# Attention weights from differences of the scan's neighbouring columns, and a new deal of the last block's side work

## The chip, the cores and the metric

The kernel runs on one core of one Trainium2 chip. The metric is the device time of one execution in microseconds (us); times are the median of several executions. TensorE (PE in the profile, PEld for its weight loads) does the matrix products, VectorE (DVE), ScalarE (ACT) and GpSimd (POOL) the elementwise work, and SyncE (SP) issues the DMA transfers.

## The reference

One layer of a hybrid decoder on x of 2048 positions by 1024 channels, in float32. x is normalised and modulated, and one input projection gives the columns of three token mixers. Their gated outputs are put side by side, go through one output projection and are added to x.

```python
proj = h @ w_in                      # columns au av az | bq bk bv bo bz bi bf | cq ck cv cz
y_a = spatial_gating_branch(ga_u, ga_v, ...) * silu(ga_z)        # branch A: 4 groups x 64
q_b, k_b = split(silu(causal_conv(concat(mb_q, mb_k))))          # branch B: mLSTM, 4 heads x 96
h_b = rms_norm(mlstm_branch(q_b, k_b, mb_v, mb_i, mb_f), ...)
y_b = sigmoid(mb_o) * h_b * silu(mb_z)
# branch C: stick-breaking attention, 6 heads x 64, for each block of 128 queries
z = einsum('bthd,bshd->bhts', qb, kb) * scale
log_not = where(strict, log_sigmoid(-z), 0.0)
suffix = cumsum(log_not, axis=3, reverse=True) - log_not
a = where(strict, exp(log_sigmoid(z) + suffix), 0.0)
outs.append(einsum('bhts,bshd->bthd', a, vb))
y_c = h_c * silu(sc_z)
x = x + gate * (concat([y_a, y_b, y_c]) @ w_out)
```

With b = sigmoid(-z) (1 where masked) and R(s) the product of b over all columns from s on, the weight of column s is sigmoid(z) times R(s+1). Since sigmoid(z) = 1 - b, that is R(s+1) - R(s).

## The kernel before

The 2048 positions are 16 tiles of 128. They are worked through in three blocks of 5, 5 and 6 tiles (`BLOCKS`). In each block the six attention heads come in three pairs (`p` = 0, 1, 2). For each pair, `c_proj` projects the pair's q, k and v for the block's tiles (a lead of some tiles first, four in the last block; the rest later), `c_evac` norms and stores them in `Kst`, `Vst` and `Qst`, and `stick` does the attention. Products are done in a split form: every operand is a rounded part and a remainder, so that one projection step of 384 columns is three matmuls (L297 to L299), eight steps to a tile.

`stick` cuts each tile's keys into units of up to four blocks of 128; a pair of the last block has 44 units. A unit goes through four steps, each one unit behind the step before it in the list. `front`: two matmuls write z into PSUM (L401, L402; two buffers), ScalarE writes bb = sigmoid(-z) (L406) and be = sigmoid(z) (L407), GpSimd sets the masked corner of the diagonal unit in bb to 1 (L409) and in be to 0 (L411), VectorE turns bb into its running product from the right (L414, a scan that carries on from the unit before), and be becomes be times bb shifted by one column (L418, in turn on VectorE and on GpSimd). `middle`: TensorE transposes be (L429) into a PSUM tile "at" (two buffers, taken in program order), ScalarE rounds it into aT (L431), VectorE writes the remainder (L432). `back`: TensorE multiplies with Vst (L444). `fin` folds the pair's two heads and sends them out.

The projections of the other branches are the side work. Each is a generator that yields after each projection step; the last block has eight such chunks of 48 steps: `bqk_proj` halves 0 and 1, `bg_proj` halves 0 and 1, `cz_proj`, `a_proj` halves 0 and 1, and `bv_proj`. `interleave` writes out the program: after each step of a pair's attention it lets the side work advance in proportion to the costs given. A scheduler that simulates the engines then sets the order on each engine, by priority among what is ready; attention has a small priority over the rest. So side work that was written late can run early, where TensorE has nothing else.

Before, the last block's chunks were dealt 3, 3 and 1 to the pairs, and `bv_proj` followed behind the last pair (`tail`). `mix` threads small work into a chunk: `gating` (branch B's gate terms for all tiles) into the first pair's side work and `first_chunk` (the first mLSTM tile) into the second's. `a_proj` keeps its gated values in two tiles with one buffer each, `va` and `gu`, which are used again by the next half, after its spatial products (L580, which take an "at" tile) and its DMA to y_d (L586).

After the last block all pools are closed, and the final part lays its tiles over their memory: the output weights are loaded into `wst` (L1026, over the projection weights `wr` and the activations `hT`) and split into `wo` (L901, L902), while mLSTM tiles and the output projection `out_proj` (L995 to L997) run.

Of the kernel before, what the change touches and what calls it, by code (L numbers as in the profile page):

```python
# [12 lines left out]
AF = mybir.ActivationFunctionType  # L13
ALU = mybir.AluOpType
# [19 lines left out]
def hybrid_block_kernel(ctx: ExitStack, tc: tile.TileContext, x, c, norm_g, w_ada, b_ada, w_in,  # L34
# [344 lines left out]
    def stick(p, t0, nb):  # L379
        units = []  # L380
        for j in range(nb):
            for h in range(2):
                s1 = t0 + j + 1
                while s1 > 0:
                    s0 = (s1 - 1) // 4 * 4
                    units.append((t0 + j, j, h, s0, s1))
                    s1 = s0
        carry = {}
        acc = {}
        outs = {}  # L390
        st = {}
        st_count = []

        def front(u):
            i, j, h, s0, s1 = u
            need[0](j)
            w = (s1 - s0) * P
            nm = f"{p}_{i}_{h}_{s0}"
            z = pz.tile([P, 512], F32, tag="z", name=f"z{nm}")
            kk = Kst[:, h, s0 * P:s1 * P]  # L400
            nc.tensor.matmul(z[:, :w], lhsT=Qst[:, j, 0, h, :], rhs=kk, start=True, stop=False)  # L401
            nc.tensor.matmul(z[:, :w], lhsT=Qst[:, j, 1, h, :], rhs=kk, start=False, stop=True)  # L402
            bb = stk.tile([P, 513], F32, tag="bb", bufs=4, name=f"bb{nm}")
            be = stk.tile([P, 512], F32, tag="be", bufs=4, name=f"be{nm}")
            nc.gpsimd.memset(bb[:, w:w + 1], 1.0)  # L405
            nc.scalar.activation(bb[:, :w], z[:, :w], AF.Sigmoid, scale=-1.0)  # L406
            nc.scalar.activation(be[:, :w], z[:, :w], AF.Sigmoid)  # L407
            if s1 == i + 1:
                nc.gpsimd.affine_select(out=bb[:, w - P:w], in_=bb[:, w - P:w], pattern=[[-1, P]],  # L409
                                        compare_op=ALU.is_gt, fill=1.0, base=0, channel_multiplier=1)  # L410
                nc.gpsimd.affine_select(out=be[:, w - P:w], in_=be[:, w - P:w], pattern=[[-1, P]],  # L411
                                        compare_op=ALU.is_gt, fill=0.0, base=0, channel_multiplier=1)
            rev = bb[:, 0:w + 1][:, ::-1]
            nc.vector.tensor_tensor_scan(rev, rev, rev, carry.get((i, h), 1.0), ALU.mult, ALU.bypass)  # L414
            carry[i, h] = bb[:, 0:1]
            eng = nc.gpsimd if len(st_count) % 2 else nc.vector
            st_count.append(0)
            eng.tensor_tensor(be[:, :w], be[:, :w], bb[:, 1:w + 1], ALU.mult)  # L418
            st[u] = [be, None]
            return 2 * w / 2.4  # L420

        def middle(u):
            i, j, h, s0, s1 = u
            nm = f"{p}_{i}_{h}_{s0}"
            be = st[u][0]
            nb_ = s1 - s0
            at = pat.tile([P, 4, P], F32, tag="at", name=f"at{nm}")
            for s in range(nb_):
                nc.tensor.transpose(at[:, s, :], be[:, s * P:(s + 1) * P], ident)  # L429
            aT = stk.tile([P, 4, 2, P], F32R, tag="aT", bufs=4, name=f"aT{nm}")  # L430
            nc.scalar.copy(aT[:, :nb_, 0, :], at[:, :nb_, :])  # L431
            nc.vector.tensor_tensor(aT[:, :nb_, 1, :], at[:, :nb_, :], aT[:, :nb_, 0, :].bitcast(F32), ALU.subtract)  # L432
            st[u][1] = aT
            return nb_ * 109

        def back(u):
            i, j, h, s0, s1 = u
            aT = st.pop(u)[1]
            if s1 == i + 1:
                acc[i, h] = pav.tile([P, 4, P], F32, tag="av", name=f"av{p}_{i}_{h}")[:, 0:2, :]  # L440
            av = acc[i, h]
            nb_ = s1 - s0
            for s in range(nb_ - 1, -1, -1):
                nc.tensor.matmul(flat(av), lhsT=Vst[:, s0 + s, h, :], rhs=flat(aT[:, s]),  # L444
                                 start=(s0 + s == i), stop=(s0 + s == 0))
            if s0 == 0:
                t1 = stk.tile([P, P], F32, tag="avs", name=f"avs{p}_{i}_{h}")
                nc.scalar.copy(t1, av[:, 1, :])
                t2 = stk.tile([P, P], F32, tag="avt", name=f"avt{p}_{i}_{h}")
                nc.vector.tensor_tensor(t2, av[:, 0, :], t1, ALU.add)  # L450
                outs[i, h] = t2
            return nb_ * 109

        def fin(u):
            i, j, h, s0, s1 = u
            if s0 != 0 or h != 1:
                return 0
            py = flat(pat.tile([P, 4, P], F32, tag="at", name=f"py{p}_{i}"))
            for hh in range(2):
                nc.tensor.matmul(py[:, hh * 64:(hh + 1) * 64], lhsT=outs.pop((i, hh)), rhs=fold, start=True, stop=True)  # L460
            yc = stk.tile([P, P], F32, tag="yc", bufs=1, name=f"yc{p}_{i}")
            nc.scalar.copy(yc, py[:, 0:P])
            nc.sync.dma_start(y_d[i * P:(i + 1) * P, 256 + p * P:256 + (p + 1) * P], yc)
            return 430

        N = len(units)
        for n in range(N + 4):
            for lag, fn in ((0, front), (2, middle), (3, back), (4, fin)):
                if 0 <= n - lag < N:
                    yield fn(units[n - lag])  # L470
# [37 lines left out]
    def bv_proj(t0, nb):  # L508
        with prio(HIGH[0]):
            wt = weights(w_in[0], [(OFF["bv"], 384)])  # L510
        for j in range(nb):
            i = t0 + j
            ps = pproj.tile([P, 512], F32, tag="proj", name=f"pv{i}")
            yield from proj_tc(ps[:, :384], wt, j, 384)
            vb = t512(f"vb{i}")
            vv = vb[:, 0:388].rearrange("p (h e) -> p h e", h=4)
            nc.gpsimd.memset(vv[:, :, 96:97], 1.0)
            nc.scalar.copy(vv[:, :, 0:96], ps[:, :384].rearrange("p (h e) -> p h e", h=4))
            nc.sync.dma_start(vb_d[i * P:(i + 1) * P, :], vb[:, 0:388])
# [230 lines left out]
    def run(g):  # L750
        for _ in g:
            pass

    def chain(*gens):
        for g in gens:
            yield from g

    def mix(a, n, g):
        for m, c in enumerate(a):
            yield c  # L760
            if m % n == n - 1:
                yield next(g, 0)
        yield from g
# [75 lines left out]
    for b, nb in enumerate(BLOCKS):  # L839
        last = b == len(BLOCKS) - 1  # L840
        chunk = nb * KT * 3 * 384 / 2.4
        HIGH[0] = 0 if b == 0 else -4000
        fillers = [
            (chain(bqk_proj(t0, nb, 0), bqk_proj(t0, nb, 1), bg_proj(t0, nb, 0)), 3),
            (chain(bg_proj(t0, nb, 1), cz_proj(t0, nb), a_proj(t0, nb, 0)), 3),
            (a_proj(t0, nb, 1), 1),
        ]
        if b == 1:
            fillers[0] = (mix(fillers[0][0], 8, gate_gemv()), 3)
        if last:  # L850
            fillers[0] = (mix(fillers[0][0], 36, gating()), 3)
            fillers[1] = (mix(fillers[1][0], 14, first_chunk()), 3)
        for p in range(3):
            lead = min(nb, 2 + b)
            if p > 0:
                ready[0] = -1
                cp = c_proj(b, t0, nb, p)
                for _ in range(lead * KT + 1):
                    next(cp)
            cp_cost = 0 if b == 0 and p == 0 else (nb - lead) * KT * 3 * 384 / 2.4  # L860
            if b == 0 and p == 0:
                HIGH[0] = -400
            if p == 2 and not last:
                get_x(t0 + nb, 0)
                get_x(t0 + nb + 1, 1)
            interleave(stick(p, t0, nb), stick_cost(t0, nb), behind(cp, fillers[p][0]), cp_cost + fillers[p][1] * chunk)
        tail = bv_proj(t0, nb)
        if last:
            run(tail)
        else:  # L870
            t1, n1 = t0 + nb, BLOCKS[b + 1]
            ready[0] = -1
            cp = c_proj(b + 1, t1, n1, 0)
            lead = min(n1, 3 + b)
            for m, _ in enumerate(chain(tail, islice(cp, lead * KT + 1))):
                j = m // KT - 1
                if 0 <= j < n1 and m % KT in (1, 5):
                    if m % KT == 1 and j + 2 < n1:
                        get_x(t1 + j + 2, j + 2)
                    hT_half(t1 + j, j, m % KT // 4)  # L880
        t0 += nb
# [200 lines left out]
```

## Time and profile before

| | |
|---|---|
| median of 3 runs | 1473.57 us (1471.72 to 1475.42) |
| the profiled execution: its own time | 1471.23 us |
| its span, first to last instruction | 1469.2 us |
| mean granted TensorE clock | 0.988 |
| busy in the span: TensorE, VectorE, ScalarE, GpSimd | 95%, 69%, 46%, 44% |

The profile is one execution. Busy time is that of an engine's instructions; matmuls overlap and their ends are modelled, so a fully busy TensorE can still have room. Idle time is put down to what released the engine. The stretches named below are in microseconds from the span's start. The last block's attention lies at 727.8 to 893.1 (pair 0), 903.4 to 1062.2 (pair 1) and 1076.3 to 1209.4 (pair 2).

### The profile page before, as it was taken

Reading aid. Unit: us, or ns where it says so; the run is one execution under the profiler, and the core shown is the slowest. Engines: PE = TensorE matmul, PEld = TensorE weight load, DVE = VectorE, ACT = ScalarE, POOL = GpSimd, SP = SyncE. Lnnn points to the kernel's source line nnn. Section 1 sums busy time; section 2 is a strip of 40 time slices with the busy share of each in tenths; the row PEclk is TensorE's granted clock in tenths of the full one; section 3 lists DMA queues with packets and bytes.
Section 4 is the critical chain, followed back from the end, with each engine's and each line's share of the span. In section 5 each row is a group of like instructions: output and inputs, shape, how many; then the busy total and the mean of one; then the engine's idle time right before and its main releaser. Section 6 shows DMA issues by size and latency. Waiting matters only on the chain.

```text
span 1469.2 us, 24957 instructions
## 1 busy us (share of the span) xinstructions
PE 1393.4 (95%) x8468; PEld 1298.2 (88%) x8468; DVE 1018.8 (69%) x1778; ACT 676.5 (46%) x1656; POOL 647.6 (44%) x1140
## 2 busy tenths in 40 slices
PE   5999999898999999999999999999999978999998
PEld 3789999798999999988999899989999867888887
DVE  6797554676995666588799976778778788444543
ACT  3364454453554444346467655556455655111110
POOL 4473553743433432554343343434445337435442
PEclk8999999999999999999999999999999999999999
DMA  9866776666535533633433344303432435555541
GB/s 324 293 204 206 237 228 197 208 202 236 191 128 176 198 116 124 222 100 127 148 105 126 104 146 137 102 15 120 157 102 69 156 113 153 178 160 154 175 154 58
DMA packets 187103, 233.19 MB, mean 159 GB/s; under 512 B 22714, under 2 KB 160344, under 8 KB 186976
## 3 DMA queue, kind: packets, MB, share of 16 engines
q1 hardware_dynamic: 186752, 231.59, 48.5%
q8 instruction: 67, 1.10, 0.3%
q14 instruction: 60, 0.49, 0.1%
q0 software_dynamic: 224, 0.02, 0.0%
HBM read 159.24 MB, written 72.31 MB: 158 GB/s over the span
## 4 chain that ended last, share of the span: by engine, by line
PE 66%; DVE 15%; DMA 6%; issue 5%; POOL 4%; ACT 2%; SPq 1%; POOLq 0%; DVEq 0%; ACTq 0%
DVE bb L414 5%; PE av L444 5%; PE at L429 4%; PE pc L297 4%; PE pc L299 4%; PE pc L298 4%; PE po L995 4%; PE po L997 3%; PE po L996 3%; PE pg L297 3%; PE pg L298 3%; PE pg L299 3%; DMA st<-in_w_in_dram 2%; PE z L401 2%; PE z L402 2%
## 5 line engine op out<-in xcount | busy, mean ns | idle before, releaser
L414 DVE TENSOR_TENSOR_SCAN bb<-bb,bb 128x513 f32<-128x513 f32 x144 | 191.3, 1328 | 25.5 <-ACT bb L406 24.7
L418 POOL TENSOR_TENSOR be<-be,bb 128x512 f32<-128x512 f32 (+3 forms) x120 | 133.0, 1108 | 132.9 <-DVE bb L414 81.4
L432 DVE TENSOR_TENSOR aT<-at,aT 128x512 fp32r<-128x512 f32 (+3 forms) x240 | 142.3, 598 | 39.8 <-ACT aT L431 39.1
L406 ACT ACTIVATE bb<-z 128x512 f32<-128x512 f32 (+3 forms) x240 | 130.2, 543 | 80.5 <-PE z L402 61.2
L444 PE MATMUL av<-aT,Vst 128*128 128x256 f32 x816 | 148.7, 295 | 17.8 <-DVE aT L432 13.0
L431 ACT CAST aT<-at 128x512 fp32r<-128x512 f32 (+3 forms) x240 | 126.6, 529 | 83.8 <-PE at L429 82.7
L444 PEld LDWEIGHTS av<-aT,Vst 128*128 128x128 f32 x816 | 119.9, 189 | 30.1 <-DVE aT L432 21.0
L429 PE MATMUL at<-ident,be 128*128 128x128 f32 x816 | 132.7, 274 | 5.2 <-DVE aT L432 2.3
L297 PE MATMUL pc<-wr,hT 128*128 128x384 f32 (+1 forms) x384 | 134.8, 355 | 2.8 <-ACT hT L290 1.3
L299 PE MATMUL pc<-wr,hT 128*128 128x384 f32 (+1 forms) x384 | 134.7, 351 | 1.6 <-DVE hT L291 1.5
L298 PE MATMUL pc<-wr,hT 128*128 128x384 f32 (+1 forms) x384 | 133.4, 347 | 0.0
L407 ACT ACTIVATE be<-z 128x512 f32<-128x512 f32 (+3 forms) x240 | 131.7, 549 | 0.0
L429 PEld LDWEIGHTS at<-ident,be 128*128 128x128 f32 x816 | 99.2, 141 | 14.2 <-DVE aT L432 3.7
L995 PE MATMUL po<-wo,yT 128*128 128x512 f32 x256 | 104.9, 410 | 0.3 <-ACT yT L984 0.3
L414 DVE TENSOR_TENSOR_SCAN bb<-bb 128x129 f32<-128x129 f32 (+3 forms) x96 | 87.1, 911 | 23.3 <-POOL bb L409 16.8
L405 POOL MEMSET bb<- 128x1 f32 x240 | 23.5, 100 | 177.6 <-DVE bb L414 123.6
L996 PE MATMUL po<-wo,yT 128*128 128x512 f32 x256 | 101.6, 397 | 0.0
L997 PE MATMUL po<-wo,yT 128*128 128x512 f32 x256 | 101.4, 399 | 0.0
L487 PE MATMUL pb<-hT,wr 128*128 128x320 f32 (+1 forms) x288 | 93.2, 324 | 1.2 <-DMA wr<-w_d 1.2
L489 PE MATMUL pb<-hT,wr 128*128 128x320 f32 (+1 forms) x288 | 92.1, 323 | 1.8 <-DVE wr L191 1.3
L297 PE MATMUL pa<-wr,hT 128*128 128x384 f32 x256 | 88.2, 347 | 5.1 <-DVE qk L360 2.4
L401 PE MATMUL z<-Kst,Qst 128*128 128x512 f32 (+3 forms) x240 | 90.2, 385 | 2.4 <-DVE Kst L371 1.6
(273 smaller groups left out, 3900.3 us busy)
## 6 DMA issues: line engine op xcount, KB each, us to landing
wr<-w_d SPq DMA_DIRECT2D x160, 384.0 KB, 5.6
w_d<-wr SPq DMA_DIRECT2D x80, 384.0 KB, 3.4
wad<-in_w_ada_dram SPq DMA_DIRECT2D x8, 1024.0 KB, 6.7
xo<-in_x_dram SPq DMA_DIRECT2D x16, 512.0 KB, 3.8
out_dram<-o SPq DMA_DIRECT2D x31, 256.0 KB, 2.9
xt<-in_x_dram SPq DMA_DIRECT2D x15, 512.0 KB, 4.9
st<-in_w_in_dram SPq DMA_DIRECT2D x60, 128.0 KB, 3.4
wr<-w_d SPq DMA_DIRECT2D x16, 392.0 KB, 6.2
```

The costliest lines, as they stand in the source:

```text
L297: nc.tensor.matmul(ps, lhsT=hT[:, 0, k, cols], rhs=wt[k][:, 0, :W], start=k == 0, stop=False)
L298: nc.tensor.matmul(ps, lhsT=hT[:, 0, k, cols], rhs=wt[k][:, 1, :W], start=False, stop=False)
L299: nc.tensor.matmul(ps, lhsT=hT[:, 1, k, cols], rhs=wt[k][:, 0, :W], start=False, stop=k == KT - 1)
L407: nc.scalar.activation(be[:, :w], z[:, :w], AF.Sigmoid)
L414: nc.vector.tensor_tensor_scan(rev, rev, rev, carry.get((i, h), 1.0), ALU.mult, ALU.bypass)
L418: eng.tensor_tensor(be[:, :w], be[:, :w], bb[:, 1:w + 1], ALU.mult)
L429: nc.tensor.transpose(at[:, s, :], be[:, s * P:(s + 1) * P], ident)
L432: nc.vector.tensor_tensor(aT[:, :nb_, 1, :], at[:, :nb_, :], aT[:, :nb_, 0, :].bitcast(F32), ALU.subtract)
L444: nc.tensor.matmul(flat(av), lhsT=Vst[:, s0 + s, h, :], rhs=flat(aT[:, s]), start=(s0 + s == i), stop=(s0 + s == 0))
L995: nc.tensor.matmul(po, lhsT=yT[:, 0, k, :], rhs=wo[k][:, 0, cs], start=k == 0, stop=False)
L996: nc.tensor.matmul(po, lhsT=yT[:, 0, k, :], rhs=wo[k][:, 1, cs], start=False, stop=False)
L997: nc.tensor.matmul(po, lhsT=yT[:, 1, k, :], rhs=wo[k][:, 0, cs], start=False, stop=k == KT - 1)
```

## The change

Two edits. In `front`, the second sigmoid and the second corner mask are gone, and be is written as the difference of two neighbouring columns of the scanned bb; the tiles, the engine that does it and its shape stay. In the last block, the side work is dealt anew: `bqk_proj` twice to pair 0; `bg_proj` twice and `cz_proj` to pair 1; `a_proj` twice and `bv_proj` to pair 2. `gating` is threaded in at every 24th step in place of every 36th. Nothing follows behind the last pair.

```diff
             nc.scalar.activation(bb[:, :w], z[:, :w], AF.Sigmoid, scale=-1.0)
-            nc.scalar.activation(be[:, :w], z[:, :w], AF.Sigmoid)
             if s1 == i + 1:
                 nc.gpsimd.affine_select(out=bb[:, w - P:w], in_=bb[:, w - P:w], pattern=[[-1, P]],
                                         compare_op=ALU.is_gt, fill=1.0, base=0, channel_multiplier=1)
-                nc.gpsimd.affine_select(out=be[:, w - P:w], in_=be[:, w - P:w], pattern=[[-1, P]],
-                                        compare_op=ALU.is_gt, fill=0.0, base=0, channel_multiplier=1)
...
-            eng.tensor_tensor(be[:, :w], be[:, :w], bb[:, 1:w + 1], ALU.mult)
+            eng.tensor_tensor(be[:, :w], bb[:, 1:w + 1], bb[:, 0:w], ALU.subtract)
...
+        if last:
+            fillers = [
+                (chain(bqk_proj(t0, nb, 0), bqk_proj(t0, nb, 1)), 2),
+                (chain(bg_proj(t0, nb, 0), bg_proj(t0, nb, 1), cz_proj(t0, nb)), 3),
+                (chain(a_proj(t0, nb, 0), a_proj(t0, nb, 1), bv_proj(t0, nb)), 3),
+            ]
...
         if last:
-            fillers[0] = (mix(fillers[0][0], 36, gating()), 3)
+            fillers[0] = (mix(fillers[0][0], 24, gating()), 2)
             fillers[1] = (mix(fillers[1][0], 14, first_chunk()), 3)
...
-        tail = bv_proj(t0, nb)
-        if last:
-            run(tail)
-        else:
+        if not last:
+            tail = bv_proj(t0, nb)
```

## Rows read from the trace of the kernel before

**Rows 1.** The page, busy time, share of the span and instructions of each engine
```profile
PE 1393.4 (95%) x8468; PEld 1298.2 (88%) x8468; DVE 1018.8 (69%) x1778; ACT 676.5 (46%) x1656; POOL 647.6 (44%) x1140
```

**Rows 2.** Busy time by stage: stretch, length, each engine (instructions), granted clock, DMA
```profile
727.80:870.70 142.90, 140.09 (x881) 134.32 (x880) 130.12 (x214) 95.80 (x203) 61.29 (x125) 1.00 0.30 99
870.70:903.40 32.70, 31.90 (x205) 30.84 (x204) 13.60 (x29) 13.73 (x34) 8.46 (x17) 1.00 0.50 163
903.40:1047.00 143.60, 140.73 (x902) 134.63 (x901) 112.95 (x179) 81.86 (x190) 60.69 (x119) 1.00 0.30 99
1076.30:1160.70 84.40, 84.12 (x532) 81.40 (x531) 66.34 (x116) 49.55 (x122) 37.24 (x81) 1.00 0.22 75
1160.70:1196.60 35.90, 27.66 (x180) 21.92 (x178) 33.55 (x43) 26.26 (x56) 15.60 (x32) 1.00 0.69 240
1196.60:1209.40 12.80, 9.25 (x62) 7.21 (x61) 10.20 (x16) 5.59 (x12) 2.45 (x2) 1.00 0.04 10
1209.40:1222.00 12.60, 10.09 (x76) 9.49 (x76) 7.67 (x13) 8.52 (x20) 7.13 (x9) 0.87 0.87 239
```

**Rows 3.** TensorE's groups of instructions in the stretch 1160.6 to 1209.4
```profile
L444 PE MATMUL av<-aT,Vst 128*128 128x256 f32 x90 | 16.8, 306 | 11.3 <-DVE aT L432 10.3 <-DVE avt L450 1.1
L429 PE MATMUL at<-ident,be 128*128 128x128 f32 x84 | 12.7, 273 | 0.0
L401 PE MATMUL z<-Kst,Qst 128*128 128x512 f32 (+1 forms) x17 | 8.0, 469 | 0.5 <-ACT be L407 0.4
```

**Rows 4.** Groups of the whole span, from the page and the groups by shape
```profile
L407 ACT ACTIVATE be<-z 128x512 f32<-128x512 f32 (+3 forms) x240 | 131.7, 549 | 0.0
L411 POOL TENSOR_SCALAR_AFFINE_SELECT be<-be 128x128 f32<-128x128 f32 x96 | 47.0, 490 | 14.5 <-ACT be L407 10.9 <-PE at L429 2.4 <-PE z L402 0.2
...
L418 POOL TENSOR_TENSOR be<-be,bb 128x512 f32<-128x512 f32 (+3 forms) x120 | 133.0, 1108 | 132.9 <-DVE bb L414 81.4
L444 PE MATMUL av<-aT,Vst 128*128 128x256 f32 x816 | 148.7, 295 | 17.8 <-DVE aT L432 13.0
```

**Rows 5.** TensorE's timeline: start, us, twelve projection matmuls apart
```profile
1147.41 0.34 PE L297 MATMUL pv<-wr,hT 128*128 128x384 f32 x1
...
1149.51 0.34 PE L297 MATMUL pv<-wr,hT 128*128 128x384 f32 x1
```

**Rows 6.** VectorE's groups: L532 at 830 to 880; L575 and the ta tile, 1072 to 1160.6
```profile
L532 DVE TENSOR_TENSOR gg<-pg,sgg 128x192 f32<-128x192 f32 x6 | 2.1, 344 | 0.8 <-ACT sgg L530 0.8
...
L575 DVE SCALAR_TENSOR_TENSOR va<-tb,rra,vn_bc 128x64 f32<-128x64 f32 x12 | 3.0, 288 | 3.7 <-POOL rra L573 3.5
...
1072.00:1160.60 88.60, 9.51 (x24) 7.70 (x24) 1.00 0.21 72
```

**Rows 7.** Attention's weighted sums in pair 0: first and last start
```profile
L444 PEld LDWEIGHTS av<-aT,Vst x172: 187/188/193, 715.8 to 893.0; 128*128 128x128 f32 x172
```

**Rows 8.** The chain of work that ended last, in order of time, around 1157
```profile
1157.06 0.24 PE z L402
1157.30 0.48 PE av L444 x4
1157.78 0.44 PE at L429 x4
```

**Rows 9.** Branch A: last projection of half 0; spatial products, first and last start
```profile
L299 PEld LDWEIGHTS pa<-wr,hT x48: 187/188/190, 1001.7 to 1044.7; 128*128 128x128 f32 x48
...
L580 PE MATMUL psp<-va,wsT x8: 484/485/487, 1062.3 to 1208.7; 128*128 128x384 f32 x8
```

**Rows 10.** bv's last matmul, output-weight loads, first use; DMA rate, 1160 to 1212 in 40 slices
```profile
L299 PE MATMUL pv<-wr,hT x48: 331/337/423, 1121.9 to 1160.7; 128*128 128x384 f32 x48
...
L901 ACT CAST wo<-wst x16: 612/614/617, 1218.3 to 1226.1; 128x512 fp32r<-128x512 f32 x16
...
L1026 SPq DMA_DIRECT2D wst<-in_w_out_dram x4: 367/381/383, 1161.0 to 1167.5; - x4
...
GB/s 0 85 280 375 336 390 432 422 422 419 413 422 404 293 298 392 408 309 297 200 36 0 0 0 0 0 0 0 17 40 0 0 0 0 0 13 0 26 213 151
```

## The prediction

> **What bounds the kernel now.** I read the page's busy times first [rows 1]: TensorE 95%, VectorE 69%, ScalarE 46%. That average hides where the 76 us of idle TensorE lie, so I cut the last block, which the change deals anew, at its pairs' attention [rows 2]. In pair 0 (727.8 to 903.4) TensorE is busy 172.0 of 175.6 us, but VectorE 130.1 of the first 142.9 us too: two engines near their limit. Pair 1 is TensorE's (140.7 of 143.6 us; VectorE 113.0). Pair 2 has two halves. To 1160.7 TensorE is full (84.1 of 84.4). There bv_proj, the last side work, is used up, and attention runs alone to 1209.4: TensorE is busy 36.9 of 48.7 us, VectorE 43.8. What ends TensorE's idle time there is one wait [rows 3]: the weighted sums L444 behind the remainder L432, 10.3 of the 11.3 us shown before that line. So this kernel is bound by TensorE nearly everywhere, by VectorE in the last 49 us of the last pair, and close to VectorE in pair 0. ScalarE bounds no stretch shown.
>
> **The weights.** The edit removes 240 sigmoids on ScalarE, 131.7 us, and 96 corner masks on GpSimd, 47.0 us [rows 4]. Neither engine sets the end anywhere above, so this time is not saved as such. What is left on the path is latency: a unit's bb and aT wait in ScalarE's queue behind other units' be, and z's PSUM tile is held by two reads in place of one. The waits of L444 bound it: 17.8 us of idle time stand before that line in the whole span, 11.3 of them in the lone stretch [rows 3, 4], where VectorE itself is the limit. So the edit is worth from 0 to 6.5 us; between the ends I take the middle, **-3**. The difference itself keeps its shape, engine and two inputs; no row shows this subtraction on GpSimd, the product takes 1.1 us [rows 4]. At half speed again (0.5 us more on every second unit) it would still hide: two units lie between it and the transpose in the list, and GpSimd is busy only 44% [rows 1]. If that cover went, the alternate units would each lose those 0.5 us of chain, part of rival 3. I take 0.
>
> The Trainium skill, page Perfetto Trace Analysis, section Identifying the Most-Contended Engine, says that a kernel gains through its most-contended engine, and that TensorE is judged by its weight loads, not by matmul busy time. Weight loads fill 88% of this span, and ScalarE is at 46% [rows 1], so by that rule the term is 0 and the sum below 3 us higher; that is rival 4.
>
> **The deal, price of a chunk.** A chunk is 6 tiles x 8 steps x 3 = 144 matmuls. Twelve take 2.10 us where they run without a gap [rows 5], so 0.175 us each and **25.2 us** a chunk on TensorE. Pair 0 loses bg_proj's first half, pair 1 swaps a_proj's first half for it, pair 2 gains that a_proj half, and bv_proj, which ran inside pair 2 already, is now written there. TensorE's total is unchanged; only its idle time can shrink. On VectorE a bg half costs 2.1 us, an a half 9.5 + 3.0 = 12.5 us [rows 6], and two spatial results of some 0.6.
>
> **Pair 0.** If TensorE alone counted it would lose 25.2 us. But VectorE keeps 130.1 - 2.1 = 128.0 us up to the last z. Its highest share in these rows is 33.55 of 35.9 us, 0.934 [rows 2]; at that share the 128 us need 137.0 in place of 142.9, **-5.9**. Behind the last z, attention took 12.8 us more when it was alone (1196.6 to 1209.4) [rows 2], and pair 1's first z came 10.3 us after pair 0's last weighted sum (893.1 to 903.4) [rows 2, 7]. So 32.7 us become 23.1, **-9.6**, if pair 1's lead projections run early in TensorE's gaps: three PSUM tiles of 4.2 us, 12.6 us, are room enough for most of that. Together **-15.5**; TensorE would then be busy 146.8 of 160.1 us. Bounds: -5.9 (the lead doesn't come forward) to -25.2. gating, threaded in earlier, is in VectorE's 130.1 us already.
>
> **Pair 1.** The same work on TensorE, 11 us less on VectorE; 2.9 us were idle [rows 2]. I take **-1** (0 to -2.9). bg's six small writes to gate_d go on SP's queue here, a_proj's two to y_d leave it; first_chunk reads rows that an earlier block wrote.
>
> **Pair 2.** The full half stays 84.4 us. The lone 48.7 us can be packed: with TensorE full, a unit's z costs 2 x 0.24, its four transposes 0.44, its four sums 0.48 [rows 8]. The counts in [rows 3], 17, 84/4 and 90/4, give 8.2 + 9.2 + 10.8 = 28.2 us; 2 us for the small products, 30.2. With the new chunk's 25.2 that is 139.8 us; pair 1's idle share of 2% adds 2.8, and the last units' chain keeps its idle time, 12.8 - 9.25 = 3.5 [rows 2]. 146.1 in place of 133.1: **+13.0**. Bounds: 28.2 gives +11, no packing (36.9) gives +19.7. VectorE has 110.1 + 13.7 = 123.8 of the 146 us, 0.85, below its limit.
>
> A new wait: a_proj's second half writes va and gu, which wait for the first half's spatial products. Those came 17.5 us after the last projection matmul [rows 9], held up because they take their "at" tile in attention's order. Behind them stand the second half's evacuations. The cover: three evacuated tiles fit the six temporaries and three more the PSUM, together all six tiles, 25.2 us of TensorE. I take 0, and some 5 us if that cover is short.
>
> **What follows.** bv_proj's last matmul frees the memory of hT and wr: the output weights are issued at 1161.0, 0.3 us later, and data flows until about 1187, 26 us; the first split is at 1218.3, 8.9 us after attention's end [rows 2, 10]. Now bv_proj will end near the last z, some 9 to 13 us before attention's end, so 26 us of loads end 4 to 8 us after the split's old place. Weights come first, and at the 400 GB/s shown 4 MB and the first tile's 1 MB take 13 us, in time; the next mLSTM tile's operands come last. I take **+1.5** (0 to 8). SP also gets bv's six writes just ahead of these loads, 0.3 us each, inside that. The clock fell behind the thin stretch: 0.87 over 12.6 us at 1209.4 [rows 2], 1.6 us of full speed lost. With TensorE full up to the last z I take **-1** (0 to -1.6).
>
> The Trainium skill, page TensorE: Matmul & The Clock Gate, section What's actually happening, has the gate halve the clock after idleness and release it with activity; the trace agrees in the 0.87 just named. By it alone the full 1.6 would come back, the sum 0.6 us lower.
>
> **Sum.** -3 - 15.5 - 1 + 13.0 + 1.5 - 1 = **-6.0 us**. The profiled execution took 1471.23 (span 1469.2 and 2.0 around it), so 1465.2; the median of runs lies 2.3 above the profiled one, and -6.0 on it gives 1467.6. I say **1467**.
>
> **Rivals.** 1 is this forecast.
> 2. *Pair 0 stays TensorE's.* With fewer instructions around it VectorE packs tighter, and the lead fills every gap: about -23.7 there, sum -14.2, **1459**. For it: VectorE's rows include stretched instructions; against: 0.934 was reached with little else to wait for.
> 3. *The idle time moves to pair 0.* Only -5.9 there: sum +3.6, **1477**. For it: 130.1 of 142.9 us.
> 4. *The weights are worth nothing*, as ScalarE ends no wait of size [rows 3]: sum -3.0, **1470.6**.
> 5. *Slower: the output weights come late.* If bv_proj ends with attention itself, the loads end 26 us after it in place of 8.9: 17 us late against the 1.5 taken, sum +9.5, **1483**. It decides from about 5 us before attention's end (13.4 of weights less 8.9). Against it: in pair 1 the side work's last matmul (1044.8) came before the last weighted sums [rows 9].
>
> **Chances.** Forecast 0.40, rival 2 0.20, rival 3 0.15, rival 4 0.15, rival 5 0.10. A measurement here tells about 0.3% (4.4 us) from no change: faster is below 1469.2, slower above 1478. The forecast, 1462 to 1472, is faster in two thirds of its cases (0.26), rival 2 always (0.20), rival 4 in 0.06: **0.52**. Rival 3 splits 0.09 and 0.06, rival 5 is slower: same **0.32**, slower **0.16**. The range 1456 to 1479 leaves out rival 5 and the far ends.
>
> **What would show it.** ScalarE near 545 us, GpSimd near 600. Pair 0's last z near 137 us after its first, with VectorE above 0.9; pair 1's first z some 15 us earlier. Pair 2 about 146 us with TensorE full to the last z, and L444's wait for L432 down from 10.3 to some 3 us. bv_proj's last matmul 9 to 13 us before attention's end and output weights in place when the split starts. Wrong if pair 0 shortens by 6 us or by 24, if pair 2 grows by 20, or if the final part begins more than 13 us after attention's end.

## The result, and the profile after

The changed kernel is slower: 1497.67 us median (1494.91 to 1498.83, 4 runs) against 1474.49 of the kernel before in the same session, a ratio of 1.016 (1.0141 to 1.0178). The forecast was 1467 and the range ended at 1479. The profiled execution took 1498.1, its span 1496.4; that of before 1471.23 and 1469.2. The 27.2 us between the spans are what has to be found.

Busy time first, the page's first part of the changed kernel, in the order of [rows 1]:

```profile
PE 1405.0 (94%) x8468; PEld 1305.9 (87%) x8468; DVE 1033.5 (69%) x1778; ACT 584.9 (39%) x1416; POOL 610.2 (41%) x1044
```

ScalarE lost 92 us and GpSimd 37, and nothing came of it. GpSimd's 610.2 is near the 600 that was named; ScalarE's 584.9 is 40 above the 545. The 131.7 us taken off there are a sum of single durations, and these overlap: before, ScalarE's durations add up to some 789 us in 676.5 us of busy time. The stages tell where the time went: the windows of the changed kernel, columns as in [rows 2]. (Its line numbers differ by up to 3 from those of before.)

```profile
727.40:858.80 131.40, 120.07 (x723) 110.59 (x721) 119.91 (x188) 71.61 (x147) 49.61 (x97) 0.96 0.25 81
858.80:898.80 40.00, 38.82 (x248) 37.41 (x248) 25.64 (x53) 17.05 (x43) 11.65 (x23) 1.00 0.46 148
898.80:1052.20 153.40, 149.11 (x953) 143.20 (x953) 115.11 (x164) 64.59 (x136) 56.24 (x108) 0.99 0.33 111
...
1058.90:1161.80 102.90, 101.39 (x628) 96.51 (x627) 91.62 (x163) 47.89 (x126) 46.55 (x88) 1.00 0.26 84
1161.80:1199.10 37.30, 35.73 (x219) 33.06 (x218) 28.01 (x42) 15.37 (x33) 10.96 (x31) 1.00 0.14 45
1199.10:1216.10 17.00, 15.49 (x111) 14.40 (x109) 9.54 (x15) 7.45 (x15) 3.41 (x5) 1.00 0.54 189
1216.10:1240.10 24.00, 11.86 (x60) 10.63 (x60) 5.16 (x10) 5.94 (x13) 6.67 (x8) 0.58 0.94 313
1240.20:1496.40 256.20, 244.29 (x1368) 207.82 (x1366) 131.13 (x231) 47.69 (x114) 114.93 (x121) 0.99 0.46 141
```

Pair 0 begins at 727.4, pair 1 at 898.8, pair 2 at 1058.9, the last weighted sum is at 1216.1 and the first matmul of out_proj at 1240.2. Before, these were 727.8, 903.4, 1076.3, 1208.6 and 1222.0: the first three are the bounds of [rows 2], within 0.4 us of each first z, and 1208.6 is the last weighted sum, ahead of the fold that ends at 1209.4. The final part before, from the last weighted sum to the end:

```profile
1208.60:1222.00 13.40, 10.89 (x80) 10.04 (x79) 8.47 (x15) 8.79 (x21) 7.13 (x9) 0.87 0.83 228
1222.00:1469.20 247.20, 239.88 (x1340) 203.75 (x1338) 123.53 (x227) 44.69 (x107) 112.73 (x118) 0.99 0.46 143
```

So the first half gave 0.4, pair 0 with what follows it 4.2 (175.6 to 171.4), pairs 1 and 2 together cost 12.1 (305.2 to 317.3), the wait from attention's end to out_proj grew by 10.7 (13.4 to 24.1), and the rest by 9.0 (247.2 to 256.2): -0.4 - 4.2 + 12.1 + 10.7 + 9.0 = 27.2. Pair 2's lone stretch is gone as meant: TensorE is busy 35.7 of 37.3 us up to the last z, where it was 27.7 of 35.9 [rows 2]. But pair 0 now has such a stretch (experiment 6).

The final part holds 19.7 of the 27.2. Four lines of the changed kernel by source line (duration, then first and last start) answer to [rows 10]: bv_proj's last matmul, the output weights' loads, their split, and the state C.

```profile
L299 PE MATMUL pv<-wr,hT x48: 331/336/636, 1162.4 to 1206.3; 128*128 128x384 f32 x48
...
L1027 SPq DMA_DIRECT2D wst<-in_w_out_dram x4: 368/381/387, 1206.6 to 1213.2; - x4
...
L902 ACT CAST wo<-wst x16: 622/626/628, 1237.8 to 1245.6; 128x512 fp32r<-128x512 f32 x16
...
L1030 SPq DMA_DIRECT2D C<-c_d x1: 368/368/368, 1226.8 to 1226.8; - x1
```

bv_proj ends 9.8 us before the last weighted sum, inside the 9 to 13 forecast, and the loads are issued 0.3 us behind it, as before. But the split starts 21.7 us behind attention's end. TensorE's timeline of the changed kernel shows what stands ahead of out_proj in its queue:

```profile
1217.59 1.09 PE L984 MATMUL pty<-ident,y 128*128 128x128 f32 x8 [0.36 <-ACT yc L459]
1226.31 2.08 PE L664 MATMUL s<-qk 96*128 96x128 f32 x8 [7.62 <-DMA qk<-qkT_d]
1228.18 0.85 PE L669 MATMUL k<-ident,qk 96*128 96x96 f32 x4
1229.68 1.61 PE L960 MATMUL c<-vbl,kw 128*96 128x97 f32 x8 [0.65 <-DVE kw L670]
1234.10 2.02 PE L947 MATMUL i<-C,qk 96*128 96x97 f32 x8 [2.81 <-DMA C<-c_d]
```

And ScalarE's timeline, what stands ahead of the split; the last line is its first one in the kernel before:

```profile
1234.68 1.28 ACT L660 ACT_TABLE_LOAD   x1 [17.14 <-DMA wT<-m_d]
1235.97 0.99 ACT L660 ACTIVATE wT<-wT,gT 128x128 f32<-128x128 f32 x3
1236.87 1.05 ACT L985 CAST yT<-pty 128x512 fp32r<-128x512 f32 x2
1237.81 2.71 ACT L902 CAST wo<-wst 128x512 fp32r<-128x512 f32 x5
...
1213.73 1.28 ACT L663 ACT_TABLE_LOAD   x1 [3.10 <-DMA wT<-m_d]
```

The scheduler put the mLSTM tiles 1 and 2 (s, k, c, i on TensorE, the gate rows wT on ScalarE) ahead of out_proj and ahead of the split. Their operands are the last of the loads. So in this order everything waits for the whole series, 313 GB/s over 24.0 us, 7.5 MB, and not for the weights alone. Before, the gate rows stood ahead of the split too, but ScalarE waited 3.1 us for them, and TensorE waited for no load between attention and out_proj.

The 9.0 us behind that have a second place. The output weights' remainders by source line, in the changed kernel and (last line) VectorE's before, and TensorE's wait list from 1195 to 1300:

```profile
L903 DVE TENSOR_TENSOR wo<-wst,wo x8: 677/988/7474, 1238.7 to 1253.4; 128x512 fp32r<-128x512 f32 x8
L903 POOL TENSOR_TENSOR wo<-wst,wo x8: 1253/1284/1752, 1239.0 to 1250.0; 128x512 fp32r<-128x512 f32 x8
...
L902 DVE TENSOR_TENSOR wo<-wst,wo x8: 675/960/1759, 1219.6 to 1234.4; 128x512 fp32r<-128x512 f32 x8
```
```profile
PE s L664 <- DMA qk<-qkT_d: 7.6, 1, 7.6
PE po L997 <- DVE wo L903: 5.0, 1, 5.0
PE i L947 <- DMA C<-c_d: 2.8, 1, 2.8
```

One remainder took VectorE 7.47 us, and TensorE stood 5.0 us behind it; before, none on VectorE took over 1.76. A further part is the order: 1368 matmuls lie behind out_proj's first one, 1340 before.

### The profile page after: what moved, and what is told of

It reads as the page before. It is cut to its first block, busy times and chain, and to the rows that moved or that the text cites. A ratio compares the mean times of both kernels' runs of the same rounds, so it can differ in the third digit from the quotient of the medians.

```text
span 1496.4 us, 24459 instructions
## 1 busy us (share of the span) xinstructions
PE 1405.0 (94%) x8468; PEld 1305.9 (87%) x8468; DVE 1033.5 (69%) x1778; ACT 584.9 (39%) x1416; POOL 610.2 (41%) x1044
## 4 chain that ended last, share of the span: by engine, by line
PE 62%; DVE 17%; DMA 8%; issue 5%; POOL 4%; ACT 2%; SPq 1%; DVEq 0%; POOLq 0%; ACTq 0%
DVE bb L411 6%; PE av L441 4%; PE po L996 4%; PE po L998 4%; PE po L997 4%; PE at L426 4%; PE pc L297 4%; PE pc L298 4%; PE pc L299 4%; PE pg L297 3%; PE pg L298 3%; PE pg L299 3%; DMA st<-in_w_in_dram 2%; DVE acc L498 2%; PE z L401 2%
## 5 line engine op out<-in xcount | busy, mean ns | idle before, releaser
L411 DVE TENSOR_TENSOR_SCAN bb<-bb,bb 128x513 f32<-128x513 f32 x144 | 195.0, 1355 | 24.1 <-ACT bb L406 21.1
L415 POOL TENSOR_TENSOR be<-bb 128x512 f32<-128x512 f32 (+3 forms) x120 | 131.2, 1094 | 143.3 <-DVE bb L411 75.9
L441 PE MATMUL av<-aT,Vst 128*128 128x256 f32 x816 | 153.5, 299 | 18.1 <-DVE avt L447 9.1
L406 ACT ACTIVATE bb<-z 128x512 f32<-128x512 f32 (+3 forms) x240 | 126.2, 538 | 98.4 <-PE z L402 48.2
L411 DVE TENSOR_TENSOR_SCAN bb<-bb 128x129 f32<-128x129 f32 (+3 forms) x96 | 90.4, 945 | 16.0 <-POOL bb L408 13.9
L484 PE MATMUL pb<-hT,wr 128*128 128x320 f32 (+1 forms) x288 | 93.4, 324 | 2.2 <-DMA wr<-w_d 2.1
L485 PE MATMUL pb<-hT,wr 128*128 128x320 f32 (+1 forms) x288 | 92.2, 322 | 0.0
L486 PE MATMUL pb<-hT,wr 128*128 128x320 f32 (+1 forms) x288 | 91.8, 322 | 0.2 <-DVE wr L191 0.2
## 6 DMA issues: line engine op xcount, KB each, us to landing
out_dram<-o SPq DMA_DIRECT2D x31, 256.0 KB, 2.6
```

Source lines behind the costliest of these rows:

```text
L415: eng.tensor_tensor(be[:, :w], bb[:, 1:w + 1], bb[:, 0:w], ALU.subtract)
```

## The experiments

Times are medians; ratios go to the kernel before, timed beside each run (1472.2 to 1473.7). Executions differ even where nothing was changed: four runs whose instructions are alike up to attention's end began block 3 at 723.1 to 727.6. So I compare stretches from their own starts, and totals by the ratios.

**1. The two edits apart.** The weights alone, and the deal alone, each on the kernel before (the diffs are the two halves of the change).

> The weights edit alone, with the deal of before. Theory A (the loss is the deal's: bv_proj's last matmul frees the memory of hT and wr some 45 us later than before, and the final part's loads start only then) expects no loss: ratio to before 0.997 to 1.001, ScalarE down by some 130 us and GpSimd by some 45, the first out_proj matmul about 13 us after pair 2's last weighted sum, as before. Rival B (the new difference disturbs the order on the engines and costs time itself) expects a good part of the 23 us: ratio 1.007 or more.

> The deal alone, with both sigmoids, both masks and the product of before. Theory A expects nearly all of the loss: ratio 1.013 to 1.019, and from pair 2's last weighted sum to the end of the span about 280 us, as in the changed kernel (260.6 before). Rival B expects ratio 1.008 or less.

Weights alone: 1474.71, ratio 1.0019 (1.0006 to 1.0032). Deal alone: 1491.18, ratio 1.0121 (1.0097 to 1.0146). The deal carries most of the loss; both ratios lie just outside what was expected. With the weights alone the final part, last weighted sum to end, is 260.7 us, as before (260.6); with the deal alone 277.6, out_proj 20.3 us behind the last sum. The same VectorE remainder is there, 7.46 us.

**2. The release held up, without the deal.** In the kernel before, the slots of hT and wr are kept by tiny GpSimd reads until a chosen unit of pair 2 has folded.

```diff
+                if (p, i, h) == (2, 15, 0):      # second kernel: (2, 14, 1)
+                    nc.gpsimd.tensor_copy(mark[:, 0:1], t2[:, 0:1])
...
+            for n, t in enumerate(wr_all[-11:]):
+                nc.gpsimd.tensor_tensor(mark[:, n + 1:n + 2], mark[:, 0:1], t[:, 0, 0:1].bitcast(F32), ALU.add)
+            nc.gpsimd.tensor_tensor(mark[:, 12:13], mark[:, 0:1], hT[:, 0, 0, 0:1].bitcast(F32), ALU.add)
```

> The kernel before, deal and weights untouched; twelve one-column GpSimd additions read hT and the last eleven wr tiles, and they wait for a mark taken when tile 15's first head is finished, about 5.7 us before the end of attention. No TensorE work is added or moved; only the memory under the output weights is held until then (1203.7 in place of 1160.7 in the trace of before). In the changed kernel the first out_proj matmul came 33.8 us after the release. Theory A expects it at about 1237 in place of 1222.0, and the time 12 to 20 us longer: ratio 1.008 to 1.014. The rival that the loads are hidden anyway, and that the loss arises inside the pairs' attention, expects ratio 0.998 to 1.003.

> The same hold, ended earlier: the mark is taken when tile 14's second head is finished (1195.2 in the trace of before, 14 us before the end of attention). Theory A expects about half the price of the longer hold: first out_proj matmul at about 1229, 5 to 11 us longer, ratio 1.003 to 1.008. A fixed cost of holding at all would show the same time as the longer hold; the rival of hidden loads expects no change.

Held to the end: 1488.04, ratio 1.0103 (1.0087 to 1.0118). Attention ends within 1.2 us of before; the loads are issued at 1206.7 in place of 1161.0, and the final part takes 277.7 us, as with the deal alone (277.6). It gets there in another way. The split and out_proj stand ahead of tile 1 here, so out_proj starts at 1225.0, not at the 1237 expected, and most of the loss lies behind its start, with more of the mLSTM tiles' work (1416 matmuls for 1340):

```profile
1209.80:1225.00 15.20, 3.37 (x14) 2.00 (x13) 4.66 (x6) 5.27 (x12) 4.52 (x4) 0.63 1.06 371
1225.00:1487.50 262.50, 252.14 (x1416) 215.15 (x1416) 128.73 (x236) 48.74 (x115) 117.71 (x125) 0.97 0.52 154
```

So a late release alone makes the final part long, in either order of the queues: the order decides where the wait falls. That the two figures agree is in part chance, because the deal has the wait behind the long remainder in it (5.1 us), and here no remainder takes over 1.82 us.

The shorter hold, loads from 1200.0, should have cost half as much and cost more: 1496.95, ratio 1.0161 (1.0145 to 1.0177), final part 284.8, with out_proj at 1238.9 and TensorE waiting 6.4 us for qk, 3.7 for C and 7.0 for yT. The last of these is the long remainder again. yT's remainder stands in VectorE's queue behind a remainder of wo that took 6.97 us while GpSimd ran five in a row; VectorE's and GpSimd's timelines:

```profile
1239.74 7.58 DVE L910 TENSOR_TENSOR wo<-wst,wo 128x512 fp32r<-128x512 f32 x2
1247.24 1.28 DVE L993 TENSOR_TENSOR yT<-pty,yT 128x512 fp32r<-128x512 f32 x2
```
```profile
1240.00 6.16 POOL L910 TENSOR_TENSOR wo<-wst,wo 128x512 fp32r<-128x512 f32 x5
```

Those 7.0 us are the difference between the two holds (7.1). That loads issued 6.7 us earlier gained nothing beside it is not explained.

**3. The release brought forward, with the deal.** The last pair's side work is written out faster than attention, so it is used up at three quarters of the pair.

```diff
-                (chain(a_proj(t0, nb, 0), a_proj(t0, nb, 1), bv_proj(t0, nb)), 3),
+                (chain(a_proj(t0, nb, 0), a_proj(t0, nb, 1), bv_proj(t0, nb)), 4),
```

> The changed kernel with the side work of the last pair written out ahead of attention's pace, cost 4 in place of 3, so that it is used up at three quarters of the pair. Theory A (the time lost lies in the late release of hT and wr): bv_proj ends 20 us or more before attention does, the final part, from attention's last weighted sum to the end, falls from 280.3 to 262 to 268 us; attention itself ends 2 to 8 us later as its last units run alone; total 1483 to 1490. Rival (the deal itself makes the final part long): the final part stays above 276 us.

1484.62, ratio 1.0072 (1.0055 to 1.0088). By source line, bv_proj's last matmul and the loads; then the windows from the last sum on:

```profile
L299 PE MATMUL pv<-wr,hT x48: 331/338/652, 1149.7 to 1191.7; 128*128 128x384 f32 x48
...
L1027 SPq DMA_DIRECT2D wst<-in_w_out_dram x4: 368/384/432, 1192.1 to 1197.8; - x4
```
```profile
1216.90:1224.40 7.50, 4.35 (x42) 4.03 (x40) 1.92 (x4) 3.79 (x9) 2.90 (x4) 0.94 0.49 155
1224.40:1479.80 255.40, 248.84 (x1384) 213.13 (x1384) 131.76 (x237) 49.84 (x118) 116.36 (x122) 0.97 0.48 144
```

bv_proj ends 25.2 us before the last sum, and the final part is 262.9 us: 17.4 of the 19.7 are back, with the deal in place, 16.6 of them ahead of out_proj. Counted as TensorE's idle time from the last sum to the end, by the windows shown, the kernel before has 9.8 us, the changed one 24.1, the first hold 22.2 and this one 9.7. Attention pays for it, 493.4 us from first z to last sum against 488.7 in the changed kernel.

**4. Less data, and another queue.** The changed kernel with one quarter of the output-weight loads (all splits read the first quarter, so it projects with other weights); and with the loads of C and of the gate rows of tiles 1 and 2 issued by ScalarE.

```diff
-        src = wst[k // 2][:, k % 2, cs]
+        src = wst[0][:, k % 2, cs]               # and wst[1] to wst[3] are not loaded
```
```diff
-    nc.sync.dma_start(C0.rearrange("p h e -> p (h e)"), c_d)
+    nc.scalar.dma_start(C0.rearrange("p h e -> p (h e)"), c_d)      # and wT<-m_d of tiles 1 and 2
```

> The changed kernel with 3 of the 4 MB of output-weight loads left out: the splits of all four quarters read the first quarter, so the output projection is computed with other weights. Theory A (amount of data behind the late release): at the 400 GB/s shown 3 MB are 7.5 us; the first out_proj matmul comes 14 to 18 us behind attention's last sum in place of 24, total 1488 to 1492. Rival B (the order of issue, not the amount): within 3 us of 24, total 1495 to 1500.

> The changed kernel, with the first load of the mLSTM state C and the gate rows wT of its tiles 1 and 2 issued from ScalarE's queue in place of SyncE's. Theory A (the 8.6 MB behind bv_proj are late as a whole; the queue's order matters little): C lands within 3 us of its old place, first out_proj matmul 22 to 25 us behind attention's last sum, total 1495 to 1500. Rival B (SyncE's queue holds C back: it was issued at 1226.8, 20 us after the first output weight): C is issued 8 us or more earlier, the first out_proj matmul comes 14 to 18 us behind attention's last sum, total 1487 to 1491.

Without 3 MB: 1488.17, ratio 1.0099 (1.0073 to 1.0124), and out_proj 16.6 us behind the last sum, where it was 24.1. The window between the two:

```profile
1212.40:1229.00 16.60, 12.08 (x61) 11.36 (x61) 5.37 (x10) 6.17 (x13) 6.10 (x7) 0.60 0.86 269
```

7.5 us less for 3 MB, what 400 GB/s gives (the mean rate of the two windows is lower, 269 and 313): the amount counts. The final part as a whole is 5.4 us shorter, 274.9. With the other queue: 1498.56, ratio 1.0177 (1.0153 to 1.0201). C is issued at 1225.3 for 1226.8, which is no earlier counted from the last sum, and out_proj stays 23.7 us behind. SyncE's queue was not the cause.

**5. The long remainder.** The changed kernel with all sixteen remainders on VectorE.

```diff
-        (nc.gpsimd if k % 2 else nc.vector).tensor_tensor(wo[k][:, 1, cs], src, wo[k][:, 0, cs].bitcast(F32),
+        nc.vector.tensor_tensor(wo[k][:, 1, cs], src, wo[k][:, 0, cs].bitcast(F32),
```

> The changed kernel, with all remainders of the output weights' split written by VectorE, none by GpSimd. Theory S (one VectorE remainder took 7.5 us while GpSimd ran five of them back to back, and TensorE stood 5.0 us behind it): no remainder on VectorE above 2 us, TensorE's idle time behind it under 1.5 us, total 4 to 6 us lower, 1491 to 1494. Rival (those 5 us are a wait for loads that another wait takes over): total within 2 us of 1497.7.

1487.26, ratio 1.0104 (1.0079 to 1.013), more than expected. By source line, and the window from out_proj's first matmul:

```profile
L903 DVE TENSOR_TENSOR wo<-wst,wo x16: 680/682/685, 1234.6 to 1245.0; 128x512 fp32r<-128x512 f32 x16
```
```profile
1236.00:1485.90 249.90, 241.81 (x1368) 206.16 (x1366) 125.92 (x239) 47.77 (x114) 111.33 (x113) 1.00 0.47 144
```

Every remainder takes 0.68 us, and what follows out_proj's start is 249.9 us for 256.2 (258.3 and 258.9 in the two runs of experiment 4, which share the split): 6.3 of the 9.0 are the shared split. The rest of the median's fall lies in the first half, where these executions differ anyway.

**6. Pair 0.** The changed kernel with bg_proj's halves in pair 0 and bqk_proj's in pair 1.

```diff
-                (chain(bqk_proj(t0, nb, 0), bqk_proj(t0, nb, 1)), 2),
-                (chain(bg_proj(t0, nb, 0), bg_proj(t0, nb, 1), cz_proj(t0, nb)), 3),
+                (chain(bg_proj(t0, nb, 0), bg_proj(t0, nb, 1)), 2),
+                (chain(bqk_proj(t0, nb, 0), bqk_proj(t0, nb, 1), cz_proj(t0, nb)), 3),
```

> The changed kernel, with both bg_proj halves in pair 0 and both bqk_proj halves ahead of cz_proj in pair 1. Theory V (pair 0 did not shorten by more than 6 us because bqk_proj's convolution and gating fill VectorE): pair 0, first z to last weighted sum, falls from 159.8 to 145 to 152 us, pair 1 (153.4) grows by 3 to 10, total 1490 to 1500. Rival (pair 0 is held by attention's own chain, whatever the side work): pair 0 stays within 3 us of 159.8.

1489.23, ratio 1.0109 (1.008 to 1.0138). Pair 0, first z to last weighted sum, in the changed kernel and then with the swap:

```profile
727.60:887.20 159.60, 147.09 (x896) 136.44 (x896) 140.26 (x227) 82.12 (x172) 57.41 (x113) 0.97 0.28 93
```
```profile
725.70:878.30 152.60, 143.08 (x896) 135.21 (x896) 115.82 (x191) 71.11 (x147) 63.99 (x114) 0.99 0.28 89
```

With 24.4 us less on VectorE the pair is 7.0 us shorter, just above the 145 to 152 expected; pair 1 grows from 153.2 to 159.7. So bqk_proj's work was a limit, but not the main one: TensorE still stands idle 9.5 us, at a VectorE share of 0.76. Of the 12.5 us that it stood idle in the changed kernel's pair 0, 8.5 lie in one stretch. TensorE's timeline has no projection matmul between these two, and the window between them reads:

```profile
798.22 0.34 PE L486 MATMUL pb<-hT,wr 128*128 128x384 f32 x1
...
825.81 0.42 PE L484 MATMUL pb<-hT,wr 128*128 128x384 f32 x1
```
```profile
798.40:825.80 27.40, 18.95 (x97) 14.96 (x96) 24.25 (x39) 17.54 (x32) 10.03 (x18) 0.81 0.01 3
```

For 27.4 us attention runs alone, with `gating` beside it, VectorE at 0.89 of the time and the granted clock at 0.81; VectorE does none of bqk_proj's convolution there. The swapped kernel has the same stretch, 26.2 us with TensorE busy 17.2, and nearly all of its idle time lies in it. In the kernel before, TensorE is busy 33.3 of the 34.0 us from 789 to 823, in which `gating` begins. So the lone stretch that the deal took out of pair 2 came up again in pair 0. No run changed the place of `gating` alone, so what made the scheduler hold the side work back is not shown.

**7. What the weights are worth.** The wait lists of VectorE, GpSimd and ScalarE with the weights edit alone have these lines:

```profile
DVE be L415 <- PE at L426: 14.5, 13, 3.7
```
```profile
POOL be L415 <- PE at L426: 44.1, 29, 5.0
```
```profile
ACT bb L406 <- DVE be L415: 23.6, 17, 3.5
ACT bb L406 <- POOL be L415: 18.8, 23, 2.3
```

GpSimd's and ScalarE's in the kernel before:

```profile
POOL be L418 <- PE at L429: 12.5, 5, 3.2
```
```profile
ACT bb L406 <- POOL be L418: 2.5, 1, 2.5
```

be's first writer had been ScalarE; now it is VectorE or GpSimd, and these stand in their queues until the transposes of an older unit have freed the buffer. Before, VectorE had no such wait, GpSimd less than a third of it, and no idle time stood before ScalarE's write (0.0, [rows 4]). So I gave be 6 buffers and bb 5 in place of 4 and 4, with the edit and without it:

```diff
-            bb = stk.tile([P, 513], F32, tag="bb", bufs=4, name=f"bb{nm}")
-            be = stk.tile([P, 512], F32, tag="be", bufs=4, name=f"be{nm}")
+            bb = stk.tile([P, 513], F32, tag="bb", bufs=5, name=f"bb{nm}")
+            be = stk.tile([P, 512], F32, tag="be", bufs=6, name=f"be{nm}")
```

> The kernel before with the edit of the weights alone, and room for more units in flight: be has 6 buffers in place of 4, bb 5. Theory W (with the edit be's writer is VectorE or GpSimd, and these two now stand in their queues until the transposes of an older unit have freed be's buffer, 14.5 and 44.1 us; before, ScalarE had taken that wait on itself, where nothing hung on it): VectorE's idle time behind the transposes falls from 14.5 under 4 us, and the kernel is 3 to 7 us faster than before, ratio 0.995 to 0.998. Rival (the edit is worth nothing because TensorE is the limit): the wait falls too, and the ratio stays at 1.000 to 1.003.

> The kernel before with the same buffers, be 6 and bb 5, and without the edit of the weights. Theory W: the buffers alone give nothing, since the wait lay on ScalarE: ratio 0.999 to 1.001. Rival (any gain of the other run comes from the buffers, not from the weights): as much faster as that run, within 1.5 us.

Both missed. With the edit: 1475.68, ratio 1.001 (0.9997 to 1.0022); VectorE's wait fell only to 7.7 us, and the 6.0 us behind a long remainder (7.59) had come up in the final part:

```profile
PE po L993 <- DVE wo L899: 6.0, 1, 6.0
```

The buffers alone: 1483.87, ratio 1.0072 (1.0052 to 1.0092), slower by 10, with the same 6.0 us wait; pair 0 there has TensorE idle 8.3 of 165 us where it was 3.6. A harmless-looking size moves the scheduler's whole order. The split was then taken off GpSimd, with the edit of experiment 5, in three kernels: weights and buffers, weights alone, neither.

> The edit of the weights alone on the kernel before, be 6 and bb 5 buffers, and all remainders of the output weights on VectorE. Theory W2 (the edit gains some 5 us, which the stall behind the shared split took back): TensorE's 6.0 us of idle time behind the remainder are gone, 4 to 7 us faster than without the move, ratio to before 0.995 to 0.998. Rival (the edit is worth nothing, TensorE is the limit): ratio 0.999 to 1.002.

> The edit of the weights alone, buffers as before (be 4, bb 4), all remainders on VectorE. There the stall was 1.8 us, so the move gives 0 to 2 us: ratio 1.000 to 1.002 under Theory W2 (be's wait on VectorE, 14.5 us, still stands) and under the rival alike. What is asked is whether the buffers matter once the stall is gone: Theory W2 says this run is 4 us or more slower than the one with more buffers, the rival says within 1.5 us.

> Control: the kernel before with all remainders of the output weights on VectorE and nothing else. Before, no remainder took over 1.8 us and TensorE did not wait for one, so both theories expect ratio 0.999 to 1.001. If it is 0.997 or less, a gain of the other two runs is the split's and not the weights'.

Ratios 0.9977 (0.9965 to 0.9989; 1468.49), 1.0002 (0.9986 to 1.0018; 1471.41) and 0.9991 (0.9981 to 1.0001; 1470.93). The first is the one version that is faster than the kernel before, by some 3.4 us. The wait behind the remainder is gone in it; its final part is 256.0 us. Against the control it is 0.14% better, which these intervals can't tell from nothing; weights without buffers gain nothing. So neither theory is held up as stated: the edit alone is worth 0, and at most some 2 us with more room.

**8. All together, with the deal:** swap, early release, VectorE's split, buffers.

> The changed kernel with all that the other runs point to: bg_proj to pair 0 and bqk_proj to pair 1, the last pair's side work at cost 4, the output weights' remainders on VectorE, be 6 and bb 5 buffers. If the terms add up: from 1497.7, 8 for the swap, 5 for the remainders, 10 for the earlier release, 4 for the buffers, 1468 to 1474, level with the kernel before. If they overlap, 1475 to 1485: then the deal has no version here that pays.

1476.53, ratio 1.0024 (1.0012 to 1.0037). The terms overlap. The final part is 261.4 us, as before the change; attention takes 492.3 us from first z to last sum, before the change 480.8. So the deal has no version here that pays.

## Why the prediction was wrong, point by point

**What follows** is the step that failed most: +1.5 for the output weights and -1 for the clock, +19.7 measured, which is 19.2 of the 33.2 us between forecast and result (pair 0 has 11.3). Its times were right (bv_proj 9.8 us before attention's end, loads 0.3 us behind it). The wrong sentence is "Weights come first ... the next mLSTM tile's operands come last", taken as if last meant harmless. In the queues of TensorE and ScalarE tile 1's instructions stand ahead of out_proj and of the split, so the last load counts; and with the other order the late series cost as much behind out_proj's start (experiment 2). [rows 10] gave 26 us of loads, and my own sum had them ending 4 to 8 us behind the split's old place; the wait grew by 10.7. The other 9.0 are not in the prediction at all; 6.3 of them are the shared split (experiment 5). Rival 5, at a chance of 0.10, had the mechanism and the sign, but its deciding point, about 5 us before attention's end, counted the weights alone; 9.8 us were not enough, 25.2 were (experiment 3).

**The clock** went the other way: 0.58 over the 24.0 us in which TensorE was half idle, against 0.87 over 12.6 [rows 2]; behind the 5.0 us wait the 128x512 matmuls take 0.63 us, the lower of the clock's two levels, in place of 0.39, and in pair 0's lone stretch it was 0.81. From the last sum on TensorE is busy 5.5 us longer than before with nearly the same matmuls (1430 for 1420). The forecast looked only at the idle time that the deal took away, not at the one it made.

**Pair 0**, -15.5, measured -4.2. Up to the last z it gained more than I took, 131.4 us for 137.0, with VectorE's share at 0.913: attention ran ahead of the side work, 27.4 us of it alone (experiment 6). Behind the last z 40.0 us stand in place of the 23.1 forecast. There TensorE is the limit, busy 38.8 us (before 31.9 of 32.7 [rows 2]); 140 of its 248 matmuls are pair 1's projections, and only 4.8 us of VectorE's 25.6 are bqk_proj's. The -9.6 was wrong in whole: the lead did not come forward, although TensorE stood idle 11.3 us ahead of the last z. Rival 3, the idle time moves to pair 0, is what happened, -4.2 for its -5.9.

**Pairs 1 and 2**: -1 and +13.0, +12.0 together; measured +12.1. Taken apart they would look wrong (-12.8 and +24.9), because pair 2's attention began earlier, with more of its own projections still to do (61 matmuls of `c_proj` behind its first z, 14 before). So only the sum was hit, not the two terms. va and gu, taken at 0, show no wait of size.

**The weights**, -3, measured -0.4 in the first half, inside the spread of executions, and +0.2% alone. Rival 4 holds; its reason, that ScalarE bounds nothing, is half of it. The other half I had not costed: with ScalarE's write gone, VectorE and GpSimd wait for be's buffer in their queues. The Trainium skill, page Perfetto Trace Analysis, section Identifying the Most-Contended Engine, would have given 0; the run agrees (ratio 1.0019).

**Sum** by the profiled spans: -0.4 (weights), -4.2 (pair 0), +12.1 (pairs 1 and 2), +19.7 (what follows) = +27.2, against -3 - 15.5 + 12.0 + 0.5 = -6.0.

What stays open: what held the side work back in pair 0, and why the lead did not come forward; why the second hold's earlier loads gained nothing (experiment 2); what the order of the queues is worth with the deal, since no run put out_proj ahead of tile 1 there; and the last 2.7 of the 9.0 us.

## What to carry to other kernels

Side work that owns memory sets when the next stage's loads may start: before moving it, find what is laid over it, sum all its loads, and look in every engine's queue for what stands behind the last of them, not the first. A stretch in which one engine idles may be paying for transfers below it; filling it is a gain only if those are still hidden. And when an operation is removed, ask which waits the next instruction on its buffer will now meet, and on which engine.

## What the runs showed of the hardware that was not expected

A subtraction with two inputs in SBUF, 0.68 us on VectorE when GpSimd has none of them, took 7.47 us while GpSimd ran five of the same kind without a gap. VectorE's and GpSimd's timelines of the changed kernel:

```profile
1241.43 11.01 DVE L903 TENSOR_TENSOR wo<-wst,wo 128x512 fp32r<-128x512 f32 x4
```
```profile
1245.09 6.19 POOL L903 TENSOR_TENSOR wo<-wst,wo 128x512 fp32r<-128x512 f32 x5
```

The first line holds four: two of 1.3 and 1.8 us, the long one from 1244.4 on, and a short one. GpSimd's five took 1.24 us each and ended at 1251.28; VectorE's long one ended 0.5 us later. In a row, GpSimd did not let VectorE in between them. The Trainium skill, page SBUF — State Buffer, section SBUF: two separate sides, says that of two such operations the one that starts first holds the shared ports for its whole length and the other is blocked; here the blocked one sat through five. It came up in eight kernels, the changed one, the deal alone, the shorter hold, both with more buffers, the swap and the two of experiment 4 (6.97 to 7.60 us), not with all on VectorE. Sharing alone does not make it: in the kernel before, with the weights alone, in the longer hold and in the early release both engines share the split, and no remainder on VectorE took over 1.82 us. That the ports are the cause is argued from this pattern; only the split on VectorE was tried.
